# When a two-layer network computes its modulation: the second layer's 32 later columns moved into the first layer's MLP

## The chip, the core and the metric

The kernel runs on one NeuronCore of a Trainium2 chip. A core has TensorE for matrix products (PE in the profile; PEld is its weight load), VectorE (DVE), ScalarE (ACT), GpSimd (POOL), and SyncE (SP), whose queue issues most DMA transfers here. Each engine works through its own list of instructions in order; semaphores make one wait for another. The metric is the device time of one execution in microseconds (us); smaller is better.

## What is computed

One inference step of two trunk layers on 384 tokens (128 of context, 256 of a latent grid) with 1024 features. Each layer turns a conditioning vector into six vectors of 1024 numbers: shift, scale and gain of the mixer, and shift, scale and gain of the MLP. There are two conditioning vectors, one for the context tokens and one for the latent tokens.

```python
def trunk_layer(x, mod, lp, cache):
    sh1, sc1, g1, sh2, sc2, g2 = jnp.split(mod, 6, axis=-1)
    h = rmsnorm(x, lp['g_norm'][0]) * (1.0 + sc1) + sh1
    m, ctx_tensors = token_mixer(h, lp, cache)
    x = x + g1 * rmsnorm(m, lp['g_norm'][1])
    h = rmsnorm(x, lp['g_norm'][2]) * (1.0 + sc2) + sh2
    f = jnp.square(jax.nn.relu(h @ lp['w_mlp1'])) @ lp['w_mlp2']
    x = x + g2 * rmsnorm(f, lp['g_norm'][3])
...
    for l in range(DEPTH):
        ...
        mod_ctx = (jax.nn.silu(c_ctx) @ w_ada[l] + b_ada[l])[None, None, :]
        ...
        mod_lat = (jax.nn.silu(c) @ w_ada[l] + b_ada[l])[:, None, :]
```

`token_mixer` has four branches (retention, a state-space branch called S5, gated linear attention, neighbourhood attention), merged by gates and projected.

## The kernel before

**Products.** Activations lie feature by feature: eight tiles of 128 features x 384 tokens. Weights come in blocks of 128 x 1024 (512 KB): for each, SyncE loads `wf`, ScalarE rounds it to the high part `wh` (L149), VectorE subtracts to get the low part `wl` (L161), and TensorE makes 24 products with it (L207 to L209: high x high, high x low, low x high). Three blocks are prepared ahead. A layer goes through the branches, the merge (`gates`, 8 blocks at a time, and `up`), the output projection (`out_proj`, 8 blocks), and the MLP in two halves, each of `mlp_up` (16 blocks) and `mlp_down` (16 blocks). At the end of `out_proj` and of the MLP stands a chain for which TensorE waits: sums of squares over the features (`tally`, with L680 on ScalarE and L684, L687 on GpSimd; then `residual`, with L735, L738, L617), then the next norm (`apply_norm`).

**The modulation.** A layer has 48 columns of 128 outputs for each of the two vectors. For one column (`ada`) SyncE loads 512 KB of `w_ada` into a place of the pool `r3` (L515), and each vector's product with it is made in one of two ways, by turns (`ada_col`): two times in three VectorE multiplies and sums in one instruction (L504), and one time in three GpSimd multiplies (L506) and ScalarE sums (L507). So three columns are four products on VectorE and two on GpSimd with ScalarE. Each writes its unneeded products into a place `j` of the pool `mid`. When a job's columns are done, L520 adds the biases; L599 makes scales and gains from them. The conditioning rows stand in the tiles `fa` and `fb` (`silu_c`).

**Jobs.** Such work is emitted one piece (one column) or two with each weight block (`step`), at lower priority; a scheduler with its own timing model then writes each engine's order. Before, the first layer's columns 16 to 33 are emitted in its merge and 34 to 39 in `out_proj`, two with each block; its columns 40 to 47 and the second layer's 0 to 15 in its MLP, one with each block; the second layer's 16 to 47 in its own merge, `out_proj` and MLP, in the same way.

**Tables.** In the same MLP two jobs make the second layer's S5 tables, from the 45th block on (`LAG1`): `s5_write`, eight tiles by six VectorE instructions each (L295 to L300), transposed on TensorE (L433), copied by ScalarE into a tile `vt` of `mid` (L434) and stored (L435); and `s5_readout`, eight tiles by six GpSimd instructions each (the same lines) with products on TensorE (L467).

**Places.** `r3` has two places and `mid` three. `s5_tables` takes two of the three when it is called, at the head of the MLP, for `bc` and `bbd`; `bc` is held until GpSimd's last table instruction that reads it, `bbd` until TensorE's last L467. That leaves one place for `j` and `vt` in the first layer's MLP:

```python
    def mid(self, shape, dt=F32):
        return self.tile("mid", shape, dt, 3)
...
        bc = self.mid([128, 2, 2, 16, 16])
...
        bbd = self.mid([128, 2, 16, 2, 16])
...
                vt = self.mid([128, 2, 2, 128])
...
            j = self.mid([128, D])
```

**The end of the MLP.** Before the last weight block but three of the second `mlp_down` every job is emitted to its end (`self.finish()` in `mlp_down`), and the second layer's first norm then reads `mod`.

Of the kernel before, what the change touches and what calls it, by code (L numbers as in the profile page):

```python
# [22 lines left out]
T = NCTX + NLAT  # L23
# [7 lines left out]
# order of the feature-major tiles of w_in: (name, first column, number of 128-column tiles)  # L31
# [3 lines left out]
# schedule: warming products per stage of residual(); columns of ada per part; priorities; engines and order of the  # L35
# residual and of the norm; weight blocks split ahead and loaded ahead; delays (in weight blocks) and rates of the jobs
# [9 lines left out]
NRAW = 3  # L46
# [7 lines left out]
# columns of the packed per-layer vector array  # L54
# [4 lines left out]
class Kernel:  # L59
# [19 lines left out]
    # --------------------------------------------------------------- tiles  # L79
# [35 lines left out]
    # ---------------------------------------------------------------- basics  # L115
# [9 lines left out]
    def split(self, hi, lo, src):  # L125
        """hi + lo = src up to the product of two low parts."""
        self.nc.scalar.copy(hi, src)
        self.nc.vector.tensor_tensor(lo, src, hi.bitcast(F32), op=SUB)  # L128

    def prefetch(self, n):  # L130
        """Issue loads and splits of queued weight blocks until n are ready."""
# [6 lines left out]
    def high(self):  # L138
        """A weight block's high parts."""
# [10 lines left out]
        if self.behind:  # the first products' results leave PSUM before  # L150
            self.no_sync(self.traced()[-1], self.behind)

    def spare_w(self):
        """Room for one more block while r3 has no other use."""
        return [self.r3([128, 1024], F32R) for _ in range(2)]

    def low(self):
        """Its low parts."""
# [6 lines left out]
    def load_raw(self):  # L165
        """Issue loads of queued weight blocks until NRAW are under way."""
# [12 lines left out]
    def start(self, job, rate=1, later=0):  # L179
        """Work to be emitted alongside the weight blocks, rate pieces with each; later > 0 lowers its priority."""  # L180
# [3 lines left out]
    def piece(self, j):  # L184
        """Emit one piece of a job; false when there is none left."""
# [12 lines left out]
    def finish(self, *jobs):  # L198
        """Emit what is left of some jobs (or of all), in turn."""
# [11 lines left out]
    def gemm_a(self, out, xs, start=True, stop=True, m=128):  # L211
        """out[m, tokens] (+)= W[:, m]^T x for one 8 x 128-row weight block; xs: 8 (hi, lo) pairs."""
# [5 lines left out]
    def gemm_first(self, xs, ordered=True):  # L218
        """Four weight blocks side by side, so that each feature tile is used as it comes; the last feature tiles one
        block after the other, so that the blocks' places come free in turn."""  # L220
# [27 lines left out]
    # ------------------------------------------------------------- constants  # L248
# [23 lines left out]
    # ------------------------------------------------- S5: token-free tables  # L272
    def exp_acc(self, out, x, n):
        """exp to float32 accuracy."""
# [17 lines left out]
    def cmul(self, eng, ore, oim, are, aim, bre, bim, shape, tmp, conj=False):  # L292
        """(ore, oim) = (are, aim) * (bre, bim); with conj, bim is minus the factor's imaginary part, and oim comes negated."""
# [8 lines left out]
    def s5_setup(self):  # L302
        """lambda powers and (lambda_bar - 1) / lambda for both layers; columns are (layer, dir, pair)."""
# [12 lines left out]
        # sin and cos of xi  # L316
# [24 lines left out]
        # powers 0..8, ascending  # L341
# [10 lines left out]
        # coef = (lambda_bar - 1) / lambda  # L352
# [16 lines left out]
        # mu = lambda_bar ** 8: (re, re), (-im, im)  # L369
# [5 lines left out]
        # read side: powers 0..8 (dir 0), 8..0 (dir 1); write side: 7..0 (dir 0), 0..7 (dir 1)  # L375
# [13 lines left out]
    def s5_part(self, l, c):  # L389
        """columns of half a tile's table: pair columns of one direction, the same among all layers'."""  # L390
# [4 lines left out]
    def s5_tables(self, l):  # L395
        """Two jobs that put one layer's write table V (transposed), read table W and the 8-token kernel's strips into
        DRAM; TensorE's part of a piece comes one piece later."""
# [1396 lines left out]
```

## Time and profile before

| what | value |
|---|---|
| time, median of 3 runs | 1556.79 us (1549.82, 1556.79, 1557.13) |
| span of the profiled execution, first to last instruction | 1547.5 us |
| own time of the profiled execution | not given apart; the fastest run is 2.3 us above its span |
| PE busy | 1436.7 us, 93% of the span |
| DVE busy | 1041.1 us, 67% |
| ACT busy | 728.9 us, 47% |
| POOL busy | 577.7 us, 37% |
| mean granted TensorE clock | 0.973 of full speed |
| idle time of PE in L209 that ended with the split L161 | 27.8 us in 24 pieces |
| L504 (product of a column on DVE), all | 106 instructions, 148.4 us |
| L506 (product on POOL), all | 54 instructions, 168.2 us |

Busy shares over the whole span hide the stages: read them by stretches of time. The first layer's MLP runs from about 520 to 800 us, the second layer's merge and output projection from about 1085 to 1240 us, its MLP from 1270 us to the end. The granted clock is 1.00 where TensorE runs at 2.4 GHz and 0.5 where it runs at 1.2 GHz.

### The profile page before, as it was taken

Reading aid. Unit: us, or ns where it says so; the run is one execution under the profiler, and the core shown is the slowest. Engines: PE = TensorE matmul, PEld = TensorE weight load, DVE = VectorE, ACT = ScalarE, POOL = GpSimd, SP = SyncE. Lnnn points to the kernel's source line nnn. Section 1 sums busy time; section 2 is a strip of 40 time slices with the busy share of each in tenths; the row PEclk is TensorE's granted clock in tenths of the full one; section 3 lists DMA queues with packets and bytes.
Section 4 is the critical chain, followed back from the end, with each engine's and each line's share of the span. In section 5 each row is a group of like instructions: output and inputs, shape, how many; then the busy total and the mean of one; then the engine's idle time right before and its main releaser. Section 6 shows DMA issues by size and latency. Waiting matters only on the chain. (4 is left out here: it accounts for less than half of the span.)

```text
span 1547.5 us, 23376 instructions
## 1 busy us (share of the span) xinstructions
PE 1436.7 (93%) x8793; PEld 1322.4 (85%) x8793; DVE 1041.1 (67%) x1490; ACT 728.9 (47%) x1361; POOL 577.7 (37%) x750
## 2 busy tenths in 40 slices
PE   6989989998887999999999999999898889999996
PEld 5867869897887899998889887789887778999996
DVE  5588933369989997647864676154989989323443
ACT  3355644434444664455444656244444446425631
POOL 4972580024556534305751019300544744000001
PEclk9989997999999999999999999799999999999999
DMA  9445323336553476634644333143556516433331
GB/s 368 141 148 184 113 83 107 128 109 231 185 199 134 130 231 217 208 127 146 197 139 158 109 114 120 48 147 109 169 187 206 181 58 215 143 123 128 131 123 55
DMA packets 95458, 234.00 MB, mean 151 GB/s; under 512 B 18065, under 2 KB 44657, under 8 KB 95345
## 3 DMA queue, kind: packets, MB, share of 16 engines
q1 hardware_dynamic: 94192, 229.33, 44.0%
q0 software_dynamic: 1152, 3.18, 0.7%
q8 instruction: 69, 1.13, 0.3%
q14 instruction: 45, 0.36, 0.1%
HBM read 217.53 MB, written 14.94 MB: 150 GB/s over the span
## 5 line engine op out<-in xcount | busy, mean ns | idle before, releaser
L161 DVE TENSOR_TENSOR wl<-wf,wh 128x1024 fp32r<-128x1024 f32 (+1 forms) x263 | 394.8, 1504 | 236.8 <-ACT wh L149 233.6
L209 PE MATMUL mm<-hh,wl 128*128 128x384 f32 (+1 forms) x1160 | 399.1, 344 | 19.5 <-DVE wl L161 19.5
L149 ACT CAST wh<-wf 128x1024 fp32r<-128x1024 f32 (+1 forms) x263 | 273.8, 1043 | 272.7 <-PE mm L208 227.1
L207 PE MATMUL mm<-hh,wh 128*128 128x384 f32 (+1 forms) x1160 | 396.8, 342 | 2.0 <-ACT fb L824 2.0
L208 PE MATMUL mm<-hl,wh 128*128 128x384 f32 (+1 forms) x1160 | 396.7, 342 | 0.0
L209 PEld LDWEIGHTS mm<-hh,wl 128*128 128x128 f32 (+1 forms) x1160 | 219.4, 189 | 31.3 <-DVE wl L161 26.2
L207 PEld LDWEIGHTS mm<-hh,wh 128*128 128x128 f32 (+1 forms) x1160 | 219.5, 189 | 7.5 <-issue 3.0
L208 PEld LDWEIGHTS mm<-hl,wh 128*128 128x128 f32 (+1 forms) x1160 | 219.4, 189 | 7.6 <-issue 5.9
L506 POOL TENSOR_TENSOR mid<-r,fa 128x1024 f32<-128x1024 f32 x27 | 82.9, 3071 | 115.1 <-DMA r<-w_ada 84.7
L209 PE MATMUL mm<-rA,wl 128*128 128x384 f32 x336 | 115.2, 343 | 8.2 <-DVE wl L161 8.2
L507 ACT ACTIVATE mid<-mid 128x1024 f32<-128x1024 f32 x54 | 57.2, 1059 | 131.3 <-POOL mid L506 131.3
L208 PE MATMUL mm<-rD,wh 128*128 128x384 f32 x336 | 115.1, 343 | 2.4 <-DVE rD L128 2.4
L207 PE MATMUL mm<-rA,wh 128*128 128x384 f32 x336 | 114.4, 343 | 2.6 <-ACT rE L680 1.9
L506 POOL TENSOR_TENSOR mid<-r,fb 128x1024 f32<-128x1024 f32 x27 | 85.3, 3158 | 59.6 <-DVE mid L504 53.8
L617 POOL TENSOR_TENSOR few<-few,negh 128x3 f32<-128x3 f32 x8 | 7.6, 954 | 248.2 <-DVE few L738 231.0
L504 DVE SCALAR_TENSOR_TENSOR mid<-r,fa 128x1024 f32<-128x1024 f32 x53 | 78.6, 1488 | 18.6 <-ACT mid L507 13.9
L504 DVE SCALAR_TENSOR_TENSOR mid<-r,fb 128x1024 f32<-128x1024 f32 x53 | 69.8, 1321 | 15.0 <-ACT mid L507 8.6
L208 PE MATMUL mm<-rC,wh 128*128 128x384 f32 x224 | 77.4, 346 | 0.0
L207 PE MATMUL mm<-rB,wh 128*128 128x384 f32 x224 | 76.1, 340 | 0.0
L209 PE MATMUL mm<-rB,wl 128*128 128x384 f32 x224 | 75.7, 338 | 0.0
L209 PEld LDWEIGHTS mm<-rA,wl 128*128 128x128 f32 x336 | 64.2, 191 | 10.8 <-DVE wl L161 10.1
L207 PEld LDWEIGHTS mm<-rA,wh 128*128 128x128 f32 x336 | 63.8, 190 | 4.8 <-ACT rE L680 2.8
(494 smaller groups left out, 2886.6 us busy)
## 6 DMA issues: line engine op xcount, KB each, us to landing
wf<-w_mlp SPq DMA_DIRECT2D x128, 512.0 KB, 3.3
r<-w_ada SPq DMA_DIRECT2D x82, 512.0 KB, 3.6
wf<-w_merge SPq DMA_DIRECT2D x64, 512.0 KB, 3.3
wf<-w_in SPq DMA_DIRECT2D x43, 512.0 KB, 3.5
wf<-w_branch SPq DMA_DIRECT2D x16, 512.0 KB, 3.9
wf<-w_out SPq DMA_DIRECT2D x16, 512.0 KB, 3.3
s_vt<-mid SPq DMA_DIRECT2D x16, 256.0 KB, 3.1
mid<-s_vt SPq DMA_DIRECT2D x8, 512.0 KB, 4.4
```

Source lines behind the costliest of these rows:

```text
L149: self.nc.scalar.copy(wh[:, :cols], raw)
L161: self.nc.vector.tensor_tensor(wl[:, :cols], raw, wh[:, :cols].bitcast(F32), op=SUB)
L207: mm(out, lh, rh, start=start, stop=False)
L208: mm(out, lh, rl, start=False, stop=False)
L209: mm(out, ll, rh, start=False, stop=stop)
L504: nc.vector.scalar_tensor_tensor(j, w, 0.5, self.cb[g], op0=MUL, op1=MUL, accum_out=o)
L506: nc.gpsimd.tensor_tensor(j, w, self.cb[g], op=MUL)
L507: nc.scalar.activation(j, j, AF.Copy, scale=0.5, accum_out=o)
L617: self.nc.gpsimd.tensor_tensor(r, src, self.negh[:, 0:3], op=ALU.pow)
```

## The change

Only the hooks that start the jobs are edited. The first layer's jobs stay as they were, except that the job of its MLP now goes on with all 48 columns of the second layer instead of 16, still one with each weight block. The second layer starts no modulation job and doesn't make the conditioning rows again. (The change also empties comment lines, which is not shown.)

```diff
-                if where == "merge":
+                if where == "merge" and l == 0:
                     self.hold()
                     self.silu_c()
                     self.start(self.ada(l, cm[l], 16, CUT1), 2, PR_BG)
-                if where == "merge2":
+                if where == "merge2" and l == 0:
                     self.hold()
                     self.start(self.ada(l, cm[l], 16 + CUT1, CUT2), 2, PR_BG)
                 if where == "out":
                     self.finish()
-                    if CUT1 + CUT2 < 24:
+                    if l == 0 and CUT1 + CUT2 < 24:
                         self.hold()
                         self.start(self.ada(l, cm[l], 16 + CUT1 + CUT2, 24 - CUT1 - CUT2), 2, PR_BG)
-                if where == "norm3":
-                    if l == 0:
-                        self.start(chain(self.ada(0, cm[0], 40, 8), self.ada(1, cm[1], 0, 16)), 1, PR_BG)
...
-                    else:
-                        self.start(self.ada(l, cm[l], 40, 8), 1, PR_BG)
+                if where == "norm3" and l == 0:
+                    self.start(chain(self.ada(0, cm[0], 40, 8), self.ada(1, cm[1], 0, 48)), 1, PR_BG)
+                    with self.background(PR_BG):
+                        for j in self.s5_tables(1):
+                            self.tables.append(self.start(chain(range(LAG1), j), 1, PR_BG))
```

What the scheduler makes of it is read from the order of the built programs; the numbers in a name tell one use of a pool from another. On VectorE, in the second layer's merge before, right behind two gated sums (`up`: L1372, L128), the splits of the next weight blocks (L161) alternate with the modulation's products (L504):

```order
L1372 TENSOR_TENSOR c1_1941_10961<-c1_1941_10961,c1_1945_10979 128x384
L128 TENSOR_TENSOR rD_1839_10478<-c1_1941_10961,rA_1838_10477 128x384
L504 SCALAR_TENSOR_TENSOR mid_1955_11008,mod_9_87<-r3_1953_11003,fb_1863_10574 128x1024
L504 SCALAR_TENSOR_TENSOR mid_1957_11012,mod_9_87<-r3_1956_11010,fa_1862_10573 128x1024
L161 TENSOR_TENSOR wl_1961_11044<-wf_1928_10905,wh_1960_11043 128x1024
L504 SCALAR_TENSOR_TENSOR mid_1964_11051,mod_9_87<-r3_1963_11049,fa_1862_10573 128x1024
L504 SCALAR_TENSOR_TENSOR mid_1965_11053,mod_9_87<-r3_1963_11049,fb_1863_10574 128x1024
L161 TENSOR_TENSOR wl_1971_11089<-wf_1939_10952,wh_1970_11088 128x1024
```

The same place after the change:

```order
L1372 TENSOR_TENSOR c1_2006_11104<-c1_2006_11104,c1_2010_11122 128x384
L128 TENSOR_TENSOR rD_1935_10692<-c1_2006_11104,rA_1934_10691 128x384
L161 TENSOR_TENSOR wl_2020_11173<-wf_1993_11048,wh_2019_11172 128x1024
L161 TENSOR_TENSOR wl_2024_11205<-wf_2004_11095,wh_2023_11204 128x1024
L161 TENSOR_TENSOR wl_2028_11237<-wf_2017_11144,wh_2027_11236 128x1024
```

The products are gone and only the splits are left. On VectorE at the end of the first layer's MLP, before the change, the split of the last MLP block (`wl_1367`) and of two blocks of the next layer stand shortly ahead of the residual's L735 and L738:

```order
L161 TENSOR_TENSOR wl_1367_7618<-wf_1357_7519,wh_1366_7617 128x1024
L1498 TENSOR_TENSOR rE_921_5051<-rE_921_5051,mm_1361_7584 128x384
L687 TENSOR_TENSOR hl_1279_7013<-hl_1279_7013 128x384 x2
L161 TENSOR_TENSOR wl_1373_7687<-wf_1365_7591,wh_1372_7686 128x1024
L161 TENSOR_TENSOR wl_1376_7717<-wf_1368_7621,wh_1375_7716 128x1024
L735 TENSOR_TENSOR hl_1279_7013<-rX_838_4536,rE_921_5051 128x384
L738 TENSOR_SCALAR few_1380_7736<-mx_1379_7726 128x3
```

After the change twelve L504 and twenty-odd table instructions stand between the last MLP block's split and L738; these are the last rows of them:

```order
L504 SCALAR_TENSOR_TENSOR mid_1404_7405,mod_9_87<-r3_1402_7400,fb_649_3609 128x1024
L474 TENSOR_TENSOR c3_1290_6897<-c3_1290_6897,mx_1423_7495 64x16
L475 TENSOR_TENSOR c3_1290_6897<-c3_1290_6897,dg_1289_6895 64x16
L504 SCALAR_TENSOR_TENSOR mid_1419_7482,mod_9_87<-r3_1418_7480,fa_648_3608 128x1024
L504 SCALAR_TENSOR_TENSOR mid_1428_7535,mod_9_87<-r3_1427_7533,fa_648_3608 128x1024
L504 SCALAR_TENSOR_TENSOR mid_1429_7537,mod_9_87<-r3_1427_7533,fb_649_3609 128x1024
L504 SCALAR_TENSOR_TENSOR mid_1436_7585,mod_9_87<-r3_1434_7580,fb_649_3609 128x1024
L504 SCALAR_TENSOR_TENSOR mid_1441_7619,mod_9_87<-r3_1440_7617,fa_648_3608 128x1024
L161 TENSOR_TENSOR r3_1466_7862<-wf_1456_7763,r3_1465_7861 128x1024
L520 TENSOR_TENSOR mod_9_87<-mod_9_87,cols_8_85 128x96
L599 SCALAR_TENSOR_TENSOR ma0_1458_7799<-mod_9_87,cols_8_85 128x16
L738 TENSOR_SCALAR few_1476_7950<-mx_1475_7940 128x3
```

L520, which needs all 48 columns, and the norm's scale `ma0` now stand in front of L738. GpSimd at the same place, before: the residual's power L617 follows small preparations of the next layer:

```order
L912 MEMSET rC_1533_8680 128x16
L913 COPY rC_1533_8680<-s5prm_32_152 128x16
L921 TENSOR_TENSOR sm_1617_9300<-rC_1533_8680,s5mu_63_308 128x64
L923 TENSOR_TENSOR sm_1618_9301<-rC_1533_8680,s5mu_63_308 128x32 x2
L617 TENSOR_TENSOR few_1381_7738<-few_1380_7736,negh_5_80 128x3
```

After the change:

```order
L298 TENSOR_TENSOR g1_1412_7426<-mid_916_5036,s5pw_64_313 128x288
L299 TENSOR_TENSOR g3_1410_7424<-g3_1410_7424,g1_1411_7425 128x288
L300 TENSOR_TENSOR g3_1410_7424<-g3_1410_7424,g1_1412_7426 128x288
L1022 MEMSET g3_1561_8531 128x6
L506 TENSOR_TENSOR mid_1403_7402<-r3_1402_7400,fa_648_3608 128x1024
L506 TENSOR_TENSOR mid_1420_7484<-r3_1418_7480,fb_649_3609 128x1024
L506 TENSOR_TENSOR mid_1435_7582<-r3_1434_7580,fa_648_3608 128x1024
L506 TENSOR_TENSOR mid_1442_7621<-r3_1440_7617,fb_649_3609 128x1024
L1280 DMA fa_1505_8203<-na_k 128x2x128
L617 TENSOR_TENSOR few_1477_7952<-few_1476_7950,negh_5_80 128x3
```

The table steps, and behind them four modulation products, now stand in front of L617 (`mid_916` is `bc`). Further up in the new order of GpSimd, which is not shown, the product `mid_1357` stands behind the residual's sum L684 of the last feature tile but one, and the product `mid_1373` and seven table instructions stand between it and L1022. On TensorE the last transposes L433 and table products L467 stand between the last MLP product and the residual's sums.

## Rows read from the trace of the kernel before

**Rows 1.** The page's part 2: busy tenths of two engines in 40 equal slices.

```profile
PE   6989989998887999999999999999898889999996
...
DVE  5588933369989997647864676154989989323443
```

**Rows 2.** Stretches: us; PE, PEld, DVE, ACT, POOL busy; PEclk; DMA share; GB/s.

```profile
525.00:600.00 75.00, 72.18 (x405) 71.80 (x405) 67.51 (x73) 49.01 (x84) 29.29 (x10) 0.98 0.73 236
...
660.00:715.00 55.00, 55.00 (x324) 54.55 (x323) 27.32 (x39) 32.83 (x54) 1.13 (x2) 1.00 0.36 125
...
717.00:767.00 50.00, 49.24 (x283) 40.57 (x283) 46.59 (x56) 21.71 (x41) 44.35 (x45) 1.00 0.53 165
...
1095.00:1185.00 90.00, 78.60 (x425) 74.26 (x424) 83.86 (x88) 39.90 (x61) 41.36 (x17) 0.98 0.62 209
...
1205.00:1240.00 35.00, 29.04 (x148) 26.82 (x146) 32.73 (x34) 19.28 (x38) 24.15 (x13) 0.95 0.43 151
...
1285.00:1320.00 35.00, 31.16 (x168) 30.20 (x167) 32.74 (x38) 22.98 (x42) 12.41 (x4) 0.95 0.57 194
...
1325.00:1425.00 100.00, 100.00 (x574) 100.00 (x573) 33.35 (x32) 38.61 (x55) 0.00 (x0) 1.00 0.36 127
```

**Rows 3.** Who TensorE waited for, 1085 to 1240 us: total, times, longest.

```profile
PE mm L209 <- DVE wl L161: 11.1, 9, 2.6
```

**Rows 4.** Timeline of GpSimd, ScalarE, VectorE: start, duration, instruction, idle before.

```profile
527.78 2.43 POOL L506 TENSOR_TENSOR mid<-r,fa 128x1024 f32<-128x1024 f32 x1 [8.30 <-DMA r<-w_ada]
...
628.05 3.27 POOL L506 TENSOR_TENSOR mid<-r,fb 128x1024 f32<-128x1024 f32 x1 [4.87 <-DVE mid L504]
...
631.35 1.06 ACT L507 ACTIVATE mid<-mid 128x1024 f32<-128x1024 f32 x1 [4.51 <-POOL mid L506]
...
632.53 1.23 DVE L504 SCALAR_TENSOR_TENSOR mid<-r,fa 128x1024 f32<-128x1024 f32 x1 [3.48 <-ACT mid L507]
...
633.80 1.22 DVE L504 SCALAR_TENSOR_TENSOR mid<-r,fb 128x1024 f32<-128x1024 f32 x1
...
635.16 3.27 POOL L506 TENSOR_TENSOR mid<-r,fa 128x1024 f32<-128x1024 f32 x1 [3.85 <-DVE mid L504]
...
649.05 1.22 DVE L504 SCALAR_TENSOR_TENSOR mid<-r,fb 128x1024 f32<-128x1024 f32 x1
```

**Rows 5.** The timeline, GpSimd, the sums of the residual in the first MLP's end.

```profile
763.49 1.48 POOL L684 TENSOR_TENSOR hl<-rX,rE 128x384 f32<-128x384 f32 x1 [0.42 <-ACT rE L680]
...
791.22 1.03 POOL L684 TENSOR_TENSOR hl<-rX,rE 128x384 f32<-128x384 f32 x1 [4.59 <-ACT rE L680]
```

**Rows 6.** The timeline, ScalarE, a table tile's copy.

```profile
746.03 0.58 ACT L434 COPY mid<-mx 128x512 f32<-128x512 f32 x1
```

**Rows 7.** Stores of table tiles, 690 to 800 us, from issue to landing.

```profile
DMA to landing us min/median/max: 2.4/3.7/5.1
```

**Rows 8.** The page's part 6: a modulation load, KB and us to landing.

```profile
r<-w_ada SPq DMA_DIRECT2D x82, 512.0 KB, 3.6
```

**Rows 9.** The timeline, VectorE and TensorE, end of the first MLP.

```profile
785.84 1.87 DVE L161 TENSOR_TENSOR wl<-wf,wh 128x1024 fp32r<-128x1024 f32 x1
...
798.03 0.33 PE L209 MATMUL mx<-rB,wl 128*128 128x384 f32 x1
...
800.09 0.15 DVE L738 TENSOR_SCALAR few<-mx 128x3 f32<-128x3 f32 x1
```

**Rows 10.** Busy time, a short stretch right after idle time; columns of Rows 2.

```profile
1245.00:1250.00 5.00, 5.00 (x33) 5.00 (x32) 3.22 (x11) 0.75 (x2) 1.42 (x3) 0.66 0.33 110
```

**Rows 11.** The timeline, VectorE, a low part of a result and two splits.

```profile
566.44 0.55 DVE L128 TENSOR_TENSOR rD<-c,rB 128x384 fp32r<-128x384 f32 x1
...
566.91 3.43 DVE L161 TENSOR_TENSOR wl<-wf,wh 128x1024 fp32r<-128x1024 f32 x1
...
572.05 1.21 DVE L161 TENSOR_TENSOR wl<-wf,wh 128x1024 fp32r<-128x1024 f32 x1
```

**Rows 12.** The timeline, GpSimd, a table step.

```profile
714.50 0.67 POOL L297 TENSOR_TENSOR g<-mid,s5pw 128x288 f32<-128x288 f32 x1
```

More of the change, by code (lines that the diff above doesn't have):

```diff
@@ L1587, in hook @@
                     self.finish()
-                    if CUT1 + CUT2 < 24:
+                    if l == 0 and CUT1 + CUT2 < 24:
                         self.hold()
                         self.start(self.ada(l, cm[l], 16 + CUT1 + CUT2, 24 - CUT1 - CUT2), 2, PR_BG)
-                if where == "norm3":
-                    if l == 0:
-                        self.start(chain(self.ada(0, cm[0], 40, 8), self.ada(1, cm[1], 0, 16)), 1, PR_BG)
-                        with self.background(PR_BG):
-                            for j in self.s5_tables(1):
-                                self.tables.append(self.start(chain(range(LAG1), j), 1, PR_BG))
-                    else:
-                        self.start(self.ada(l, cm[l], 40, 8), 1, PR_BG)
+                if where == "norm3" and l == 0:
[3 more added lines that the diff above has]
+                            self.tables.append(self.start(chain(range(LAG1), j), 1, PR_BG))
             hs = self.layer(l, hs, hook, first)
```

## The prediction

> **What bounds the kernel now.** I began with the page's shares by slice: PE is at 9 tenths in most slices, DVE in some [rows 1]. So TensorE is the bound over long stretches, and what matters is where it isn't. The view by stretches shows that. From 1325 us on, in the second layer's MLP without modulation, TensorE is busy 100.00 of 100 us with 574 matrix instructions, 0.174 us each, so a block of 24 takes 4.2 us; VectorE needs only 33.35 us there [rows 2]. In the second layer's merge, 1095 to 1185 us, with the modulation beside it, VectorE is busy 83.86 of 90 us and TensorE only 78.60 [rows 2]. The view of waits says for whom TensorE waited there: 11.1 us for splits of weight blocks on VectorE [rows 3]. The modulation's products stand between the splits, so they are what makes the splits late. In the first layer's MLP, 660 to 715 us, where before nothing else runs, TensorE is full with VectorE at 27.32 of 55 us [rows 2]: that is the room into which the change moves 32 columns. From 717 to 767 us the tables fill VectorE (46.59 of 50) and GpSimd (44.35), and TensorE still gets 49.24 [rows 2].
>
> **What is taken away.** 32 columns are 64 products, some 43 on VectorE and 21 on GpSimd and ScalarE, with 32 loads and their places in SyncE's queue. The gain is the time that TensorE lost beside them. 1095 to 1185 us: 90 - 78.60 = 11.4 us idle, and at a mean granted clock of 0.98 another 90 x 0.02 = 1.8. The output projection, 1205 to 1240: 35 - 29.04 = 6.0 and 35 x 0.05 = 1.8. The MLP's begin, 1285 to 1320: 35 - 31.16 = 3.8 and 1.8. Together 26.6 us [rows 2]. Some of it isn't the modulation's: `up` has waits of its own. I take 25 us. Bounds: the wait for splits alone, with the half-clock time and the MLP's part, about 18; all of it and a little of the residual behind it, 28. The conditioning rows that are no longer made a second time lie beside full TensorE stretches, so I cost them at nothing; without that cover they would be a few us.
>
> **What is added: the chain on one place.** Before, the 24 columns in the first layer's MLP ran strictly one after the other. In the timeline a product on GpSimd (2.43 us alone, 3.27 beside VectorE) is followed by ScalarE's sum (1.06), then VectorE's product (1.23) and its next (1.22), then GpSimd's next begins [rows 4]. That is what one free place in `mid` makes of it. The first begins at 527.78, the last VectorE product ends at 649.05 + 1.22 = 650.27: 48 products, 16 such rounds of three, 122.5 / 16 = 7.66 us a round, 5.1 us a column [rows 4]. 56 columns are 37 rounds. The order of the built program puts 100 of the 112 products on that one place, and five table tiles `vt` between them, each of which holds it for the copy (0.58) [rows 6] and the store to its landing (median 3.7) [rows 7].
>
> Up to the second `mlp_down` that is hidden: 82 products are 27.3 rounds, 527.8 + 27.3 x 7.66 = 737 us, while the L684 behind them on GpSimd waits for a feature tile that TensorE finishes some ten us later. From there the chain goes with TensorE's pace, since products and L684 alternate on GpSimd, and the fourth L684 starts at 763.49 [rows 5]. What follows is a walk in the new order with durations of before:
>
> 763.5, L684 1.5, L687 1.2: 766.2. Then up to `mid_1373`, on one place: four GpSimd products with ScalarE's sum and the read of the accumulator, 4 x 3.8 = 15.2; six VectorE products, 6 x 1.3 = 7.8; four table tiles, 4 x 4.3 = 17.2. That gives 806.4, and some 5 us for instructions of others that stand between in the same queues (sums, gains, table steps, L735), so 811.4. Its ScalarE part runs beside what comes next: seven table steps on GpSimd at 0.67 to 0.85 [rows 12], 5.3 us, from 810.2: 815.5. Then TensorE's last table products, which need two more `vt` copies to free PSUM: 5.5, 821. Only then `bbd` is free and the last group starts: two GpSimd products in turn with their sums, 2 x 3.8 = 7.6; a VectorE product, 1.3; the last load of `w_ada`, which needs its place in `r3`, 3.6 [rows 8] and its issue 0.3; the last GpSimd product and sum, 2.4 + 1.3; L520 and L599, 0.4. That is 837.9. L738 stands behind, and ran at 800.09 before [rows 9]. **The tail: 38 us**, in which TensorE has nothing but table products, because its last MLP product ended at 798.03 and its blocks' splits at 785.84 + 1.87 [rows 9] don't come later than before.
>
> Bounds of the tail. Below: even if all ahead were free, `mid_1357` stands behind the L684 at 791.22 [rows 5] and small steps of 4 us, so from 796 on 13 us to the end of `mid_1373`, 5.3 of table steps and 16 for the last group: 830, and with the shortest landing (2.4) twice 828, a tail of 28. Above: rounds as slow as beside tables and splits throughout, 60.
>
> **Two small losses.** In the first `mlp_up` with columns TensorE was busy 72.18 of 75 us at clock 0.98 [rows 2], a loss of 2.8 + 1.5 = 4.3; the second `mlp_up` had no loss and now gets the same columns. The chain has slack there, so I take 2 (0 to 4.3). And behind a wait of 40 us TensorE starts at the lower level: 0.66 in the 5 us behind a wait [rows 10], 1.7 us; before, the clock was full at this place. I take 2 (0 to 4). The 32 loads, now between the loads of the MLP's weights, find SyncE's queue with a block every 4.2 us and a load of 3.6; I cost them at nothing, as they did for the 24 columns; if they weren't covered, each late block would cost TensorE up to 3.6 us.
>
> **The sum.** -25 + 38 + 2 + 2 = +17 us. On the profiled execution's span, 1547.5, that is 1564.5. Its own time isn't given; the fastest run, 1549.82, lies 2.3 us above the span and the median, 1556.79, 9.3. I forecast the median: 1556.8 + 17 = **1574 us**. What a measurement of this kernel can tell from no change is about 0.5%, 7.8 us.
>
> **The rivals.** (a) *VectorE and GpSimd get in each other's way, and TensorE itself falls behind in the second `mlp_up` and beside the tables.* A split took 3.43 us beside a GpSimd product and 1.21 alone [rows 11]. If such pairs never overlap, a block of `mlp_up` needs 1.21 for its split, 0.55 for a low part [rows 11] and 0.86 columns x (4/3 x 1.3 + 2/3 x 2.43 = 3.35): 4.6 against 4.2 us, 16 blocks lose 7 us; and in the twelve blocks beside the tables, where both engines are full already, 0.75 columns x 3.35 = 2.5 us a block make 30, less the 12 of three blocks prepared ahead, 18. With 25 us more, +42: 1599 us. For it: the split of 3.43. Against: the first `mlp_up` lost 4.3, and in 717 to 767 the busy times of both engines sum to 90.9 us of 50 [rows 2], so much of it does overlap or is waiting that hurts nobody. The Trainium skill, "SBUF — State Buffer", section "Who interferes with whom", speaks for this rival: a VectorE instruction with two inputs in SBUF and a GpSimd instruction that reads SBUF exclude each other for the whole of the one that started first. By that rule taken strictly the time would be that of (a); the split of 3.43 agrees with it, the table stretch doesn't show how far it holds for short steps.
>
> (b) *The other side: a table tile gives its place back at its copy, not at the landing.* Then each of the four before `mid_1373` and the two behind it costs 0.6 instead of 4.3: six times 3.7 is 22 us, the tail 16 and, without the small losses, 25 - 16 = 9 us faster: 1548. It decides from about 1 us of holding a tile on. Against it: the store reads the tile until it is done, and the L684 at 791.22 stays where it is, which alone keeps some 28. I see nothing in the trace for it, since the stores of before lie further apart than their landings.
>
> (c) *The tail is as short as its lower bound and the gain as large as 28*: 28 - 28, and the small losses: no change, about 1557 to 1560.
>
> That the columns are not moved at all is no rival: the second layer's order has no product left.
>
> **Chances.** The forecast, with its own range of +8 to +32: 0.58, all slower. (a) and what lies between: 0.17, slower. (c) and the forecast's lower end: 0.20, no change. (b) and like it: 0.05. So faster 0.05, same 0.20, slower 0.75. The range leaves out half of (a) and of (b): -4 to +40, 1553 to 1597 us.
>
> **What would show it.** In the profile after: between 1095 and 1185 us on before's clock TensorE busy nearly all the time and VectorE near 45 of 90; no L504 in the second layer. At the end of the first MLP a gap of TensorE of some 30 to 40 us with a granted clock below 1, L738 near 838, the last L506 just ahead of it, GpSimd and VectorE taking turns as in [rows 4] and ScalarE's L434 between them. Rival (a) would show as long waits of TensorE for splits between 660 and 790 us. The prediction is wrong if L738 comes before 822 (then the gain is larger than the loss), or if TensorE in the second layer's merge keeps waiting.

## The result, and the profile after

The change makes the kernel slower: 1573.44 us in the median of 4 runs (1571.76 to 1576.19), against 1555.20 us for the kernel before (1549.82 to 1557.13); ratio 1.0131, 95% interval 1.0108 to 1.0154, or +18.2 us. The profiled execution has a span of 1574.4 us (1547.5 before).

Part 2 of the page after, busy tenths of TensorE and VectorE and tenths of the granted clock in 40 slices of 39.4 us, answers to [rows 1].

```profile
PE   6979989998887999997963999989999999999996
...
DVE  5589933468989996799985657634344695323433
PEclk9999998999999999999985999979999999999999
```

TensorE has a new hole in the slices 21 and 22 (787 to 866 us), the end of the first MLP, with the clock down to 5 tenths; and the second layer's merge, slices 30 to 32, is now at 9. The stretches (us; PE, PEld, DVE, ACT, POOL busy; clock; DMA share; GB/s) answer to [rows 2]; the second layer's merge and output projection lie at other times than before.

```profile
660.00:715.00 55.00, 53.30 (x300) 51.52 (x300) 52.55 (x57) 37.81 (x65) 20.89 (x7) 1.00 0.66 215
717.00:767.00 50.00, 41.27 (x228) 39.32 (x227) 49.93 (x51) 23.42 (x40) 33.18 (x22) 0.93 0.56 185
...
825.00:850.00 25.00, 7.86 (x38) 4.93 (x38) 15.25 (x22) 6.03 (x13) 21.27 (x18) 0.50 0.54 172
850.00:875.00 25.00, 14.01 (x67) 13.20 (x68) 18.00 (x39) 7.97 (x14) 16.80 (x12) 0.64 0.49 171
...
1144.00:1284.00 140.00, 138.47 (x802) 136.41 (x801) 86.38 (x105) 57.30 (x89) 40.14 (x31) 1.00 0.41 136
```

Three things are to be seen. In 1144 to 1284 us TensorE is full: that is the gain. In 717 to 767 us it falls to 41.27 of 50, from 49.24 [rows 2], with VectorE at 49.93: TensorE waits *before* the tail, where the forecast had it on time. And in 825 to 850 us it is nearly idle at the lower of its two clock levels. The timeline at the MLP's end answers to [rows 9].

```profile
813.81 0.33 PE L209 MATMUL mx<-rB,wl 128*128 128x384 f32 x1
...
815.29 2.52 POOL L506 TENSOR_TENSOR mid<-r,fa 128x1024 f32<-128x1024 f32 x1
...
857.12 3.33 POOL L506 TENSOR_TENSOR mid<-r,fb 128x1024 f32<-128x1024 f32 x1
...
862.16 0.16 DVE L738 TENSOR_SCALAR few<-mx 128x3 f32<-128x3 f32 x1
```

The MLP's last product ends 15.8 us later than before, and L738 follows it by 48 us where it followed by 2. The waits (engine, line, who was waited for; us in total, times, longest): the first two lines are of 660 to 815 us, the third of 815 to 863 us, the last is VectorE's from 690 to 865 us.

```profile
PE mm L209 <- DVE wl L161: 8.4, 7, 3.3
PE mx L433 <- DVE c L474: 4.4, 1, 4.4
...
PE mm L699 <- ACT r L149: 14.1, 1, 14.1
...
DVE mid L504 <- DMA s_vt<-mid: 6.5, 3, 3.1
```

**The balance by stretches.** I cut every kernel at the same instructions: the first L722 of a residual (x takes the sum) and the first L1372 of the second layer's merge (the sum of `up`). "Start" is L722 behind the first layer's output projection. All are in us and of the profiled executions; "time" is the median.

| kernel | start | first MLP | branches 2 | merge + out_proj 2 | MLP 2 | time |
|---|---|---|---|---|---|---|
| before | 500.0 | 303.6 | 282.4 | 165.0 | 286.4 | 1551 to 1555 |
| the change | 503.1 | 363.9 | 282.6 | 134.3 | 280.2 | 1573.4 |
| e1 gain alone | 499.9 | 303.6 | 284.0 | 134.3 | 280.4 | 1515.5 |
| e2 price alone | 498.1 | 361.6 | 284.1 | 166.8 | 285.9 | 1609.1 |
| e3 junk apart | 502.5 | 356.3 | 276.8 | 134.2 | 281.5 | 1567.6 |
| e4 junk and vt apart | 498.0 | 367.8 | 284.9 | 134.3 | 280.4 | 1578.7 |
| e5 change, all on VectorE | 488.0 | 324.1 | 285.3 | 134.3 | 280.4 | 1521.6 |
| e6 the same, vt apart | 482.7 | 317.5 | 285.3 | 134.3 | 280.5 | 1513.1 |
| e7 before, all on VectorE | 486.5 | 299.4 | 283.0 | 148.9 | 281.5 | 1508.6 |
| e8 24 moved, VectorE | 482.9 | 313.5 | 276.9 | 134.3 | 281.5 | 1509.3 |
| e9 e5 + GpSimd's products | 484.5 | 395.5 | 285.1 | 134.3 | 280.4 | 1591.3 |
| e10 16 moved, VectorE | 482.8 | 300.6 | 285.2 | 134.3 | 280.3 | 1495.7 |
| e11 24 moved, tables later | 482.7 | 306.6 | 281.4 | 134.3 | 280.2 | 1504.7 |
| e12 16 moved, with GpSimd | 502.0 | 319.8 | 283.0 | 139.1 | 285.1 | 1537.6 |

The change gains 30.7 us in merge and out_proj and 6.2 in the second MLP, and pays 60.3 in the first. Each kernel has one profiled execution here: the spans of the first two lie 26.9 us apart and their medians 18.2, and "start", which this change does not touch, lies between 498.0 and 503.1 us in the seven kernels whose first layer's merge shares its products with GpSimd, so differences of a few us in this table mean little.

### The profile page after: what moved, and what is told of

Its sections match the earlier page's. It is cut to its first block, busy times and chain, and to the rows that moved or that the text cites. A ratio compares the mean times of both kernels' runs of the same rounds, so it can differ in the third digit from the quotient of the medians.

```text
span 1574.4 us, 23360 instructions
## 1 busy us (share of the span) xinstructions
PE 1435.8 (91%) x8793; PEld 1329.3 (84%) x8793; DVE 1030.6 (65%) x1484; ACT 727.2 (46%) x1359; POOL 572.6 (36%) x750
## 4 chain that ended last, share of the span: by engine, by line
PE 45%; DVE 11%; POOL 6%; issue 4%; DMA 2%; ACT 2%; SPq 0%; DVEq 0%; POOLq 0%; ACTq 0%
PE mm L208 12%; PE mm L207 12%; PE mm L209 12%; DVE wl L161 2%; DVE mid L504 2%; DVE hl L785 1%; POOL mid L506 1%; POOL sm L923 1%; DMA s_vt<-mid 1%; POOL rC L929 1%; POOL sm L921 1%; POOL sm L924 1%; DMA r<-w_ada 1%; PE my L960 1%; DVE rD L128 1%
## 5 line engine op out<-in xcount | busy, mean ns | idle before, releaser
L161 DVE TENSOR_TENSOR wl<-wf,wh 128x1024 fp32r<-128x1024 f32 (+1 forms) x263 | 372.2, 1418 | 265.0 <-ACT wh L149 261.8
L209 PE MATMUL mm<-hh,wl 128*128 128x384 f32 (+1 forms) x1160 | 397.4, 343 | 10.8 <-DVE wl L161 10.7
L149 ACT CAST wh<-wf 128x1024 fp32r<-128x1024 f32 (+1 forms) x263 | 273.7, 1043 | 276.9 <-PE mm L208 224.9
L209 PEld LDWEIGHTS mm<-hh,wl 128*128 128x128 f32 (+1 forms) x1160 | 218.8, 189 | 20.6 <-DVE wl L161 15.6
L507 ACT ACTIVATE mid<-mid 128x1024 f32<-128x1024 f32 x54 | 57.2, 1059 | 149.5 <-POOL mid L506 149.5
L209 PE MATMUL mm<-rA,wl 128*128 128x384 f32 x336 | 115.9, 345 | 8.3 <-DVE wl L161 8.3
L506 POOL TENSOR_TENSOR mid<-r,fa 128x1024 f32<-128x1024 f32 x27 | 79.6, 2947 | 103.3 <-DMA r<-w_ada 54.5
L617 POOL TENSOR_TENSOR few<-few,negh 128x3 f32<-128x3 f32 x8 | 7.6, 952 | 286.5 <-DVE few L738 269.9
L504 DVE SCALAR_TENSOR_TENSOR mid<-r,fa 128x1024 f32<-128x1024 f32 x53 | 76.5, 1445 | 31.2 <-ACT mid L507 13.9
L504 DVE SCALAR_TENSOR_TENSOR mid<-r,fb 128x1024 f32<-128x1024 f32 x53 | 71.6, 1352 | 19.9 <-ACT mid L507 14.8
L209 PE MATMUL mm<-rB,wl 128*128 128x384 f32 x224 | 76.1, 340 | 2.0 <-DVE wl L161 2.0
L209 PEld LDWEIGHTS mm<-rA,wl 128*128 128x128 f32 x336 | 64.9, 193 | 9.6 <-DVE wl L161 9.6
L1370 POOL TENSOR_TENSOR c<-c,c 128x384 f32<-128x384 f32 x16 | 17.1, 1067 | 148.8 <-DVE c L1368 117.2
```

What stands on the lines that cost most here:

```text
L149: self.nc.scalar.copy(wh[:, :cols], raw)
L161: self.nc.vector.tensor_tensor(wl[:, :cols], raw, wh[:, :cols].bitcast(F32), op=SUB)
L209: mm(out, ll, rh, start=False, stop=stop)
L504: nc.vector.scalar_tensor_tensor(j, w, 0.5, self.cb[g], op0=MUL, op1=MUL, accum_out=o)
L506: nc.gpsimd.tensor_tensor(j, w, self.cb[g], op=MUL)
L507: nc.scalar.activation(j, j, AF.Copy, scale=0.5, accum_out=o)
```

## The experiments

**Gain and price apart.** e1 is the change without the 32 columns, which are then computed nowhere (those parts of the modulation hold their bias alone); e2 is the kernel before with all 48 columns in the first MLP and the 32 computed once more in the second layer.

```diff
# e1, on the change
-self.start(chain(self.ada(0, cm[0], 40, 8), self.ada(1, cm[1], 0, 48)), 1, PR_BG)
+self.start(chain(self.ada(0, cm[0], 40, 8), self.ada(1, cm[1], 0, 16)), 1, PR_BG)
+b = cm[1][0][:, C_BADA + 16:C_BADA + 48].unsqueeze(2).to_broadcast([128, 32, 2])
+nc.vector.tensor_copy(cm[1][1][:, 16:48], b)
# e2, on the kernel before
-self.start(chain(self.ada(0, cm[0], 40, 8), self.ada(1, cm[1], 0, 16)), 1, PR_BG)
+self.start(chain(self.ada(0, cm[0], 40, 8), self.ada(1, cm[1], 0, 48)), 1, PR_BG)
```

> The 32 columns of the second layer's modulation are left out of the first MLP as well, so that they are computed nowhere (those parts of the modulation hold their bias alone). What is left is the gain without its price. Theory from the trace of the changed kernel (merge and out_proj 30 us shorter, MLP 7 us shorter): 37 us less than the kernel before, 1518 us. By the prediction's term (25 us, from the busy time of TensorE): 1530 us. The first MLP should end with its residual at 800 us, as in the kernel before.

> The kernel before, with the second layer's 48 columns in the first MLP as in the change, while the second layer computes its 32 columns again in its merge and MLP as before. What is left is the price without the gain. Theory from the trace of the changed kernel (the first MLP with its tail 58 us longer): 1613 us. By the prediction's terms (38 + 2 + 2): 1597 us. The second layer's merge should take 166 us as before; a merge shorter than that would say that part of the gain is something else than the columns leaving.

Measured: e1 1515.48 us, 36.3 less than the runs of the kernel before beside it (1551.77; ratio 0.9776, 0.9758 to 0.9794). e2 1609.11, 57.3 more (1.0380, 1.0361 to 1.0400). The two add up to +21.0, near the change's +18.2, so gain and price nearly add up, and both are larger than the prediction's terms (25 and 42).

**Is the tail the one free place of `mid`?** e3 gives VectorE's unneeded elements a place of their own; e4 gives `vt` one too.

```diff
# e3 and e4
             if (turn + g) % 3 < 2:
+                j = self.mid([128, D]) if self.junk is None else self.junk
                 nc.vector.scalar_tensor_tensor(j, w, 0.5, self.cb[g], ...
             else:
+                j = self.mid([128, D])
                 nc.gpsimd.tensor_tensor(j, w, self.cb[g], op=MUL)
...
                 if where == "norm3" and l == 0:
+                    self.junk = self.tile("rs", [128, 768]).bitcast(mybir.dt.bfloat16)[:, 0:D]
# e4 only, for the second layer's tables
-                vt = self.mid([128, 2, 2, 128])
+                vt = self.tile("u8", [128, 768])[:, 0:512].rearrange(...)
```

> The changed kernel, with one difference: the products of VectorE in the first MLP, whose elements nobody reads, are written (as bfloat16) to a place of their own, so that only GpSimd's products and the tables' transposed parts use the one free place of mid. The work stays the same. Theory 'one place' (the tail is the chain of products that wait for each other on that place): VectorE no longer waits for ScalarE, the job follows its pace of a column per weight block, the last column is done before the last product of the MLP, the tail of 46 us shrinks to under 8 and the time falls to 1533 us (1522 to 1545). Rival 'too much work' (VectorE and GpSimd have 56 columns, the tables and the splits to do and get in each other's way): the work is the same, the tail stays at 30 us or more and the time at 1560 to 1578.

> As the run before it, and the transposed parts of the write table (vt) have a place of their own too, so that the one free place of mid is GpSimd's alone. Theory 'one place': the 3 to 5 us that each landing of vt holds the place fall away as well; 1528 us (1518 to 1540), at most 8 us less than with vt in mid, since the job then has slack. Rival 'too much work': as with the run before, 1560 to 1578. A rival 'the landing of vt is the whole of it': this run is 20 us or more under the one before it.

Measured: e3 1567.59 us (ratio 1.0112, 1.0087 to 1.0138), e4 1578.68 (1.0176, 1.0138 to 1.0214). My theory fell, though not in its mechanism. In e3's timeline the tail is gone: L738 (L740 in this kernel) stands 2.06 us behind the last product, as before the change.

```profile
853.20 0.33 PE L210 MATMUL mx<-rB,wl 128*128 128x384 f32 x1
...
855.26 0.15 DVE L740 TENSOR_SCALAR few<-mx 128x3 f32<-128x3 f32 x1
```

But that last product now stands at 853.20 and not at 813.81. The time has moved from behind TensorE to within it: its wait for the splits (L162 here), 520 to 870 us, first e3, then e4:

```profile
PE mm L210 <- DVE wl L162: 26.8, 19, 4.5
```

```profile
PE mm L210 <- DVE wl L162: 35.7, 26, 4.5
```

In the change itself it was 8.8 over the same window. So the one place was a brake as well as a queue. What the products do to TensorE once it is open is, by the prediction's rival (a), an effect of GpSimd on VectorE, which I then tested by itself.

**GpSimd's products against VectorE's.** e5 and e7 change one line of the change and of the kernel before; e6 is e5 with `vt` apart as in e4; e9 is e5 with GpSimd's products of the first MLP made once more for nobody.

```diff
# e5 (on the change), e7 (on the kernel before)
-            if (turn + g) % 3 < 2:
+            if True:
                 nc.vector.scalar_tensor_tensor(j, w, 0.5, self.cb[g], ...
# e9, besides (self.junk as in e3)
+                if self.junk is not None and (turn + g) % 3 == 2:
+                    nc.gpsimd.tensor_tensor(self.junk, w, self.cb[g], op=MUL)
```

> The changed kernel, with all products of the modulation (the first layer's merge included) on VectorE and none on GpSimd and ScalarE; the places of mid are as in the change. Theory 'GpSimd in VectorE's way' (with the places apart the tail went to TensorE, which waited for the split L161: a split takes 1.2 us by itself and 3.4 us where a GpSimd product lies over it): 37 products of the first MLP less on GpSimd spare VectorE up to 37 x 2.2 = 81 us and cost it 37 x 1.3 = 48 us, and nothing waits for ScalarE any more; the first MLP ends with its residual at 820 to 830 us and not 862, and the time is 1538 us (1525 to 1552). Rival 'too much work for VectorE' (it is busy 9 tenths of the first MLP): a third more products on it make TensorE wait longer, and the time is 1580 us or more.

> As the run before it, with a place of its own for the transposed parts of the write table (vt), so that VectorE never waits for a landing with splits queued behind its product. Theory 'GpSimd in VectorE's way': up to 8 landings of 2.4 to 5.1 us leave VectorE's path, 3 to 12 us less than the run before it, 1530 us. Rival 'too much work for VectorE': the same as the run before it within 5 us.

> The kernel before, with all products of the modulation on VectorE. Theory 'GpSimd in VectorE's way': part of what the second layer's columns cost in its merge (splits of 1.9 us in the mean there, 1.2 us by themselves, and TensorE waiting 11 us for them) is GpSimd's; merge and MLP get shorter and the time is 1540 us (1530 to 1550). Rival 'too much work for VectorE': 1560 us or more, and TensorE's wait for the split in the second layer's merge grows over 11 us.

> The changed kernel with all products on VectorE (the first of the runs with them there, 1522 us), and beside them, in the first MLP alone, GpSimd computes again the products that were its own, into a scratch place that nobody reads; ScalarE has no part and no product waits for them, only the load into their place of r. Theory 'GpSimd in VectorE's way': the 37 products put up to 37 x 2.2 us back on VectorE's splits; their mean in the first MLP goes from 1.29 us to 1.5 or more, TensorE waits for them again, the first MLP gets 25 to 80 us longer and the time is 1550 to 1600 us. Rival 'the turns with ScalarE on the one place': 1522 us within 8.

Measured: e5 1521.56 us (0.9793, 0.9766 to 0.9820), e6 1513.06 (0.9742, 0.9710 to 0.9774), e7 1508.55 (0.9726, 0.9701 to 0.9751), e9 1591.30 (1.0248, 1.0228 to 1.0268). Half as many products again on the engine that seemed full, and the first MLP is 39.8 us shorter (363.9 to 324.1); the rest of e5's gain is 15.1 us in the first layer's merge, whose products are on VectorE too. Putting the GpSimd products back, with nobody waiting for their results, makes the first MLP 71 us longer (324.1 to 395.5). Neither ScalarE's sums nor the place can explain that, since e9's extra products have no part in them; nor can late loads, since VectorE stood idle for `w_ada` 5.9 us ahead of its products in e9 and 15.3 in e5 (530 to 830 us); nor can GpSimd's own table steps coming late, for which TensorE waited 2.1 us in e9 and 4.6 in e5 (490 to 870 us). e5 and e7 went further than I had said, e6 is 8.5 us under e5 as its theory had it. TensorE's wait for splits, 490 to 870 us, in e5 and then in e9, and the stretch from L722 to the last product of the first MLP, again in e5 and then in e9 (columns of [rows 2]):

```profile
PE mm L209 <- DVE wl L161: 7.4, 6, 3.9
```

```profile
PE mm L210 <- DVE wl L162: 39.0, 21, 4.9
```

```profile
487.95:800.85 312.90, 290.51 (x1652) 281.07 (x1652) 286.91 (x431) 139.12 (x228) 84.21 (x78) 0.98 0.65 210
```

```profile
484.47:864.91 380.44, 314.35 (x1652) 295.75 (x1652) 367.64 (x432) 138.97 (x228) 193.84 (x110) 0.93 0.53 174
```

So 67.5 of the 71 us lie before the last product: TensorE is idle 66.1 us there and not 22.4, and the lower mean clock costs most of the rest.

How one product does it is seen in e9's timeline (L507 is GpSimd's product, L162 the split, L505 VectorE's product; start, duration):

```profile
582.15 3.45 POOL L507 TENSOR_TENSOR rs<-r,fa 128x1024 bf16<-128x1024 f32 x1 [10.41 <-DMA r<-w_ada]
...
583.26 3.42 DVE L162 TENSOR_TENSOR wl<-wf,wh 128x1024 fp32r<-128x1024 f32 x1
...
585.68 3.25 POOL L507 TENSOR_TENSOR rs<-r,fb 128x1024 bf16<-128x1024 f32 x1
...
586.61 3.41 DVE L505 SCALAR_TENSOR_TENSOR mid<-r,fb 128x1024 f32<-128x1024 f32 x1
```

In these rows the two engines take strict turns. GpSimd's product alone takes 2.4 us and VectorE's split or product 1.2 ([rows 4], [rows 11]). The first GpSimd product begins just after a VectorE product (582.11 to 583.34) and takes 3.45; the split that begins at 583.26 takes 3.42 and ends 1.08 us after GpSimd's end at 585.60; the next GpSimd product takes 3.25, and VectorE's next one, begun at 586.61, ends 1.09 us after that. A busy VectorE in [rows 2] was in part a waiting one. The Trainium skill, "SBUF — State Buffer", section "Who interferes with whom", says it: a VectorE instruction with two inputs in SBUF and a GpSimd instruction that reads SBUF shut each other out for the whole of the one that came first. These rows agree, in both orders and for both kinds of VectorE instruction. And "GPSIMD Engine Reference" of the Trainium skill, section "Engine selection", puts elementwise work on VectorE, since GpSimd is about half as fast with two inputs; 2.4 against 1.2 us agrees with that too.

e7 tells what of the second layer's price was GpSimd's. In its merge and out_proj (1068 to 1218 us) the splits take 1.409 us in the mean:

```profile
L161 DVE TENSOR_TENSOR wl<-wf,wh 128x1024 fp32r<-128x1024 f32 x31 | 43.7, 1409 | 1.0 <-ACT wh L149 0.9
...
PE mm L209 <- DVE wl L161: 1.7, 2, 1.5
```

and in the kernel before (1085 to 1252 us) 1.896, with TensorE's wait of 11.1 [rows 3]:

```profile
L161 DVE TENSOR_TENSOR wl<-wf,wh 128x1024 fp32r<-128x1024 f32 x31 | 58.7, 1896 | 1.3 <-ACT wh L149 1.3
```

The stretch goes from 165.0 to 148.9 with all columns still in it: 16.1 of the 30.7 us that the move gains were GpSimd's. The other 14.6 stay, some 10 of them in out_proj (from the last L1372 to L722, 1172.6 to 1217.7 in e7, 45.1 us, against 35.0 without columns), where TensorE waits 3.8 us for the last split, which VectorE makes behind the last columns' products.

But GpSimd's turns are not the whole of the change's loss. With every product on VectorE the move of all 32 columns still loses: e5 (1521.56 us, 0.9766 to 0.9820) is slower than e7 (1508.55, 0.9701 to 0.9751), since it gains 15.7 us behind the first MLP and pays 24.7 in it. With `vt` apart as well (e6) the two can't be told apart.

**How many columns to move.** e8 moves the 24 of merge and out_proj and leaves the MLP's 8, e10 moves 16 and leaves 8 at the merge's begin and 8 in the MLP, both on VectorE (e8 with `vt` apart); e11 is e8 with later tables; e12 is e10 with GpSimd's share.

```diff
# e10 (e12 without the first change)
-            if (turn + g) % 3 < 2:
+            if True:
...
+if where == "merge" and l:
+    self.hold()
+    self.silu_c()
+    self.start(self.ada(l, cm[l], 32, 8), 2, PR_BG)
+if where == "norm3" and l:
+    self.start(self.ada(l, cm[l], 40, 8), 1, PR_BG)
-    self.start(chain(self.ada(0, cm[0], 40, 8), self.ada(1, cm[1], 0, 48)), 1, PR_BG)
+    self.start(chain(self.ada(0, cm[0], 40, 8), self.ada(1, cm[1], 0, 32)), 1, PR_BG)
# e8: silu_c at "merge2" without columns, and ada(1, cm[1], 0, 40); e11 also
-LAG0, LAG1 = 2, 44
+LAG0, LAG1 = 2, 50
```

> As the second of these runs, but only the 24 columns of the second layer's merge and output projection are moved; the 8 of its MLP stay there. Theory 'GpSimd in VectorE's way': the 8 columns cost little in the second MLP once GpSimd does not do a third of them (7 us before), and the first MLP has 8 columns (21 us of VectorE) less: 1525 us, the fastest so far. Rival 'too much work for VectorE': 8 columns less in the first MLP make its end 8 x 2 x 1.3 = 21 us earlier than in the run before it, which itself is slow: 1560 us.

> The changed kernel with all products on VectorE and 16 columns moved: those of the second layer's columns 32 to 39 are computed in its merge and 40 to 47 in its second MLP; the places of mid are as in the change. The job in the first MLP has 40 columns and ends before the tables begin (44 blocks), so neither meets the other: first MLP 299.5 us from residual to residual as with the kernel before on VectorE alone, merge and out_proj 134 to 140 us (149 there), second MLP 281. Theory 'the price is where columns and tables meet': 1496 us (1490 to 1503). Rival 'each column has its price in the first MLP' (24 columns cost 14 us there, so 16 cost 9): 1505 us.

> The kernel with 24 columns moved, all on VectorE (1509 us; its first MLP is 14 us longer than with none moved, and TensorE is busy 39 of 50 us from 700 to 750), with one number changed: the tables begin 50 weight blocks into the first MLP and not 44, when the 48 columns are done. Theory 'the price is where columns and tables meet': the first MLP is 8 to 14 us shorter, 1498 us (1492 to 1505). Rival 'each column has its price': no change, 1509; rival 'later tables run into the end of the MLP': 1515 or more.

> As the kernel with 16 columns moved, but with the products shared among VectorE, GpSimd and ScalarE as in the change: the same columns at the same places, one line different. It tells how much of the change's loss is the number of columns and how much the engine. 40 columns at 5.1 us (7.66 us a round of 1.5 columns) take 204 us and end near the begin of the tables, so there is no tail behind the MLP, but splits of 3.4 us under 27 GpSimd products. Theory 'GpSimd in VectorE's way, and the tail comes from the columns over 40': first MLP 308 to 318 us (305 before), merge and out_proj 146 us (16 of 24 columns of a gain of 30), second MLP 288 as before; 1540 us (1532 to 1550), some 45 us over the same columns on VectorE alone. Rival 'the number of columns alone': within 10 us of those 1496. Rival 'the tail comes at any number over 24': 1560 or more.

Measured: e8 1509.28 us (0.9719, 0.9688 to 0.9750), e10 1495.73 (0.9637, 0.9620 to 0.9654), e11 1504.67 (0.9690, 0.9670 to 0.9710), e12 1537.57 (0.9911, 0.9896 to 0.9926). e10 came out as forecast, in its time within a microsecond and in its stretches (300.6, 134.3, 280.3): with 40 columns in the first MLP the job is over before the tables fill VectorE, and 717 to 767 us is full, which it was not in the change.

```profile
660.00:715.00 55.00, 54.24 (x322) 50.86 (x323) 49.94 (x79) 28.89 (x50) 20.40 (x22) 1.00 0.56 184
717.00:767.00 50.00, 50.00 (x281) 44.02 (x280) 39.30 (x46) 23.08 (x39) 30.97 (x31) 1.00 0.58 193
```

e8 missed my number (1525) because the kernel before on VectorE is itself so much faster; against that one (e7) its 24 columns gain 14.6 and pay 14.1 in the first MLP. In e11, where columns and tables no longer overlap as much, that price falls to 7.2, which is 6.9 us less where its theory said 8 to 14, and the branches behind are 4.5 us longer than in e8, so its time is not clearly other than e8's (the intervals meet). e12 shows the two causes together: with the same 16 columns and GpSimd's share the time is 42 us over e10's, and still 0.9% under the kernel before. Its first MLP is a little longer than I had said (319.8 us for 308 to 318), its merge shorter (139.1 for 146), probably because the columns that stay there are done early and none is left for out_proj. So the change fails by its last 16 columns, and most of all where GpSimd takes its turns; fewer columns were worth moving even so. e10 is the fastest of all, faster than both kernels: 0.9637 of the kernel before.

## Why the prediction was right, point by point

The time (1574 forecast, 1573.4 measured), its sign and the place of the loss were right. That +17 and +18.2 lie so close is luck, a balance of two errors: the gain is 11 to 12 us larger than its term, the price 15 to 18 us.

*What bounds the kernel.* Right that TensorE waits for splits in the second layer's merge. "The modulation's products stand between the splits, so they are what makes the splits late" was half of it: with more products between them, all of them on VectorE (e7), the wait falls from 11.1 to 1.7 us.

*The gain, 25 us: mis-sized; 36.3 by e1, 36.9 by the stretches.* The step summed TensorE's idle time and clock in three windows. For merge and out_proj that is 11.4 + 1.8 + 6.0 + 1.8 = 21.0 [rows 2], and 30.7 went. The windows left out the seams between them: over the whole of 1085.9 to 1251.0 TensorE is busy 143.2 of 165.1 us and the mean clock of 0.97 costs some 5 more, 27 together. The rest is in TensorE's own busy time: the same 770 instructions are busy 143.2 us before and 132.8 in the change (the first line is of the kernel before), twice what the clock explains.

```profile
1085.90:1251.00 165.10, 143.18 (x770) 134.86 (x771) 151.12 (x169) 72.29 (x120) 89.39 (x45) 0.97 0.53 182
```

```profile
1149.60:1283.87 134.27, 132.82 (x770) 131.08 (x770) 81.58 (x98) 56.12 (x88) 38.11 (x29) 1.00 0.42 138
```

Counting products would have done: 31 blocks (7 of `up`, 16 of `gates`, 8 of `out_proj`) x 24 x 0.174 us [rows 2] = 129.5, and 5.3 from the last product to L722 (1278.5 to 1283.9 in the change), 134.8, against 134.3 measured. The MLP's 5.6 was nearly right (6.2). The upper bound of 28 was too low for the same reason.

*The tail, 38 us with TensorE on time: the chain was right, its start and its length were not.* Its parts are in the trace as told: the place is handed from engine to engine, and e3 takes the tail away by opening the place. But the walk had 74.4 us from the fourth L684 (763.5) to L738 (837.9), and it took 87.8, from 774.35 to 862.16. From `mid_1357`, which the prediction's lower bound puts at 796, to 838 are 42 us; it took 815.29 to 862.16, 46.9, and began 19 us later. L738 came 62 us later than before and not 38: 46 by the tail and 16 because the last product was late.

*The small loss in the second `mlp_up`, 2 us (0 to 4.3): right in size; what failed is "its blocks' splits don't come later than before" and TensorE on time beside the tables.* From its first to its last product with a low part (L209) the second `mlp_up` takes 69.7 us for 66.4 (650.47 to 720.16; before 647.13 to 713.53). For the products behind it, beside the tables, the sum had nothing. Of the 15.8 us by which the MLP's last product is later, 3.7 are already there at L738 of the first output projection (495.23 and 498.96), ahead of anything that the change moves. At the end of the ninth of the 16 blocks of `mlp_down` TensorE is still only 3.1 us late (the first line is of the kernel before, the second of the change; the third is the change's stretch behind it, columns of [rows 2]):

```profile
767.70 0.33 PE L209 MATMUL mm<-rA,wl 128*128 128x384 f32 x1
```

```profile
770.84 0.34 PE L209 MATMUL mm<-rA,wl 128*128 128x384 f32 x1
...
771.00:815.00 44.00, 36.07 (x201) 33.36 (x200) 39.22 (x49) 20.90 (x39) 25.89 (x23) 0.92 0.53 168
```

But in the kernel before all table products are done by then (the last L467 starts at 766.55), and in the change most are still to come. The last seven blocks take 43.0 us (770.84 to 813.81) for 30.3: of that stretch 4.4 us are a table transposition (L433) that TensorE's list holds in front of the next products, which waits for VectorE's L474, and 2.0 are waits for splits; the clock of 0.92 costs 3.5. The slack of the chain is no slack of VectorE: in the rows above a GpSimd product costs VectorE's next instruction up to 2.2 us.

*The half clock, 2 us: right.* From L738 to L722 it took 4.8 us after and 3.4 before, with the clock at 0.64 in 850 to 875 us.

*The loads at nothing: right.* From 520 to 870 us VectorE's splits waited 0.8 us in all for ScalarE's high parts, and the waits of ScalarE's casts (L149) name no load.

*Rival (a)* had the right mechanism and too small a chance. It is worth up to 12 us in the change, where the single place holds the products apart, up to 39 to 47 us more in e3 and e4, where nothing does (their last products at 853.2 and 860.3 against 813.8), and, as e9 makes likely, most of the 42 us between e7 and the kernel before. My objection, that the busy times of both engines summed to 90.9 of 50 us in the table stretch, was read wrongly: an instruction that is shut out counts as busy. *Rival (b)* is refuted: VectorE's products waited 6.5 us, three times, for the landing of `vt`. *Rival (c)* had both terms too small.

## What to carry to other kernels

Before moving work in time, ask which engine should do it: here one line that takes products off GpSimd is worth 42 us to the kernel before, and the move 13 at best on top of that, with half of the columns (e7 to e10). What a stretch can gain is better counted from its number of products at the full rate than from the idle time shown (30.7 us here, for 21.0 summed). A resource that holds a chain back may also be what keeps it from harming others, so freeing it has to be weighed with what then meets.

## What the runs showed of the hardware that I had not expected

A GpSimd product and a VectorE split or product, each with two inputs in SBUF (the on-chip memory), don't run side by side: 3.4 us where VectorE alone takes 1.2, 3.2 to 3.5 where GpSimd alone takes 2.4, and both are counted as busy. Their busy shares, 90.9 of 50 us together [rows 2], say nothing of work done side by side. 38 GpSimd products whose results nobody uses made a stretch of 324 us 71 us longer, 1.9 us each.

What stays open: the second layer's branches take 277 to 285 us in kernels that have the same work there; e3 and e8 lie at the lower end, and I have not found why. Nor was it tried to take the tables' GpSimd steps off that engine too.
